# First layer of a four-layer net: half of the shift row and V's shift rows computed by streaming the weights through TensorE, the norm done tile by tile, three weight tiles' products interleaved

## Chip, cores and metric

One core of a Trainium2 chip. The metric is device microseconds (us) of one execution of the whole program, the median of several.

## The reference

A block of two layers (attention with a Hyena mixer, then a pooling layer) is followed by a block of two other layers; all of it is float32, with 512 rows of width 1024 and 256 context rows. The change touches the first layer only, up to the attention scores. Cut to that:

```python
def _modulate(h, shift, scale):
    return h * (1 + scale) + shift
...
    s_lat = jax.nn.silu(c)
    s_ctx = jax.nn.silu(c_ctx)
...
        mod_l = [m[:, None, :] for m in jnp.split(s_lat @ ada_w[i] + ada_b[i], N_MOD, axis=-1)]
        a_lat = _modulate(_rmsnorm(h_lat, norm1_g[i]), mod_l[0], mod_l[1])
...
            mod_c = jnp.split(s_ctx @ ada_w[i] + ada_b[i], N_MOD, axis=-1)
            a_ctx = _modulate(_rmsnorm(h_ctx, norm1_g[i]), mod_c[0], mod_c[1])
...
            p_lat = a_lat @ mix_w_in[e] + mix_b_in[e]
            q_l = _axial_rope(_split_q(p_lat), row, col)
            k_l, v_l = _split_kv(p_lat[..., KV_START:HY_START])
            k_l = _axial_rope(k_l, row, col)
...
            att_l = _diff_post(_diff_attn_blocked(q_l, k_all, v_all, lam), subln_g[e], lam_init)
            hy_l = _hyena(p_lat[..., HY_START:], hy_conv_w[e], hy_conv_b[e], _hyena_filter(seq_len, *filt), hy_bias[e])
```

So a row "shift" of 1024 numbers, once for the 512 rows (c) and once for the context (c_ctx), comes from a vector of 1024 times a 1024 x 1024 matrix. Q, K, V and the Hyena inputs come from the normed rows, the scores from Q and K after the rope.

## The kernel before, in words

The program is one long list of work that the class `Prog` writes out in order for each engine; each engine takes its own instructions in that order, and waits where an operand isn't there. PE multiplies, ACT scales, casts and evacuates PE's banks, VectorE (DVE in the profile, `V` in the code) and GpSimd (POOL, `G`) do the rest, SP issues the transfers. A table `PR` says which of V, G and A (ACT, with POOL adding) does an operation, and how many steps of a side job are put in at each place.

Weights come through six raw tiles of 128x1024. `_dma_to` (line 226, transfers at L233) issues them in a fixed order; `_done_part` asks for the one six places on, once the writing of one tile's last user is behind. A weight tile is cast by ACT to its high part (L255), and the rest is its low part (L273, on V or G by `PR` or `l_eng`). `prefetch` and `consume` put these operations out ahead of the products by `look` parts. A product of float32 accuracy is three matmuls in the fast type, high by high, low by high, high by low (`mm3`, L458 to L460). The modulation rows of later places (`_ada_step`) stand between the weights in the same stream: rows scaled by a column of numbers (`scaled`, L371 on POOL, L373 on ACT) and added (`add_scaled`, L378 on V, L383 on POOL).

The first layer begins with `start`. Its eight column strips of the modulation matrix give the scale `gg` (L1015). `groups` multiplies each of eight tiles of the input, scaled by `gg`, with V's weights (V before its row factors and its shift), 18 matmuls a tile. Side jobs are put between the groups: `hyena_hidden` (two small products with a sine), `first_shift`, and `hyena_filter`. `first_shift` makes the shift: all 16 half rows of eight raw tiles are scaled and added up into four accumulators (two halves, c and c_ctx), the first half on POOL, of the second the c part on V and the c_ctx part by ACT and POOL; then 32 matmuls with a column of ones (L1104) sum over the partitions, and two additions give `sh` (L1107).

The norm comes next. The row factor is broadcast and copied to SBUF; V multiplies eight tiles by it (L1120), ACT applies scale and shift to give the high part (L1129), POOL or V computes the same again (L1130), V takes the difference as low part (L1124). The eight context tiles go the same way at half the width (L1141 to L1144). `v_shift` then makes V's row of shift times weights on V and on ACT and POOL (L378, L383, steps set by `vsj`), broadcasts it with a matmul by ones (L1169), adds the bias (L1170), and adds the row to V's six tiles (L1181).

In `layer0`, Q's first tile is multiplied and roped; then for j = 0 to 3 a K tile is multiplied with the rows and then with the context, and roped. `rope` evacuates the bank on ACT (L1462), shuffles on V (L1463), multiplies by the tables (L1465, L1466) and adds (L1467). The stacking of a K (`stack`, casts and differences L1438 to L1446) is put off by one `defer`. `fj` puts in steps of the Hyena filter (its low parts L527, its products L619), `vsj` steps of `v_shift`. Behind the loop come the scores (L1500, L1505), whose maxima V takes (L1501), for s = 0, 1 and so on, with the other Q and Hyena products between them.

## Time and profile before

| | us |
|---|---|
| median of 3 runs | 2603.05 (2602.36 to 2605.51) |
| the profiled execution | 2603.6 |
| its span in the trace | 2601.4 |
| PE busy | 2455.8 (94%) |
| DVE busy | 1798.1 (69%) |
| POOL busy | 1393.9 (54%) |
| ACT busy | 1178.6 (45%) |
| the stretch up to 437 us: PE / DVE busy | 333.65 / 382.69 |
| behind it (2164.40 us): PE / DVE busy | 2122.11 / 1415.43 |

The span is the time from the first to the last instruction in the trace; the run's time has 2.2 us more around it. A busy time is the sum of an engine's instructions, waits not counted. Matmuls are pipelined, so their starts tell more than their durations. The granted clock is TensorE's, as a share of 2.4 GHz (0.50 is 1.2 GHz).

### The profile page before, as it was taken

Reading aid. Unit: us, or ns where it says so; the run is one execution under the profiler, and the core shown is the slowest. Engines: PE = TensorE matmul, PEld = TensorE weight load, DVE = VectorE, ACT = ScalarE, POOL = GpSimd, SP = SyncE. Lnnn points to the kernel's source line nnn. Section 1 sums busy time; section 2 is a strip of 40 time slices with the busy share of each in tenths; the row PEclk is TensorE's granted clock in tenths of the full one; section 3 lists DMA queues with packets and bytes.
Section 4 is the critical chain, followed back from the end, with each engine's and each line's share of the span. In section 5 each row is a group of like instructions: output and inputs, shape, how many; then the busy total and the mean of one; then the engine's idle time right before and its main releaser. Section 6 shows DMA issues by size and latency. Waiting matters only on the chain.

```text
span 2601.4 us, 31958 instructions
## 1 busy us (share of the span) xinstructions
PE 2455.8 (94%) x11496; PEld 2053.2 (79%) x11496; DVE 1798.1 (69%) x2614; ACT 1178.6 (45%) x2180; POOL 1393.9 (54%) x1104
## 2 busy tenths in 40 slices
PE   7787887999999899999999999999999999999998
PEld 6566666888888788888778888888887788888887
DVE  6899987786656787766678776455477876743334
ACT  3446553554443633333676644222257764523131
POOL 6686747287761389973475437878137544230001
PEclk9888998999999999999999999999999999999999
DMA  7232423276782267663322326667333123343331
GB/s 247 85 122 89 136 69 96 69 208 201 203 235 82 58 171 212 213 197 92 91 67 63 105 86 191 187 173 209 107 91 91 53 82 115 114 139 96 95 89 49
DMA packets 433366, 330.28 MB, mean 127 GB/s; under 512 B 11799, under 2 KB 365207, under 8 KB 433208
## 3 DMA queue, kind: packets, MB, share of 16 engines
q1 hardware_dynamic: 429976, 322.22, 41.6%
q0 software_dynamic: 3232, 6.03, 0.8%
q8 instruction: 90, 1.47, 0.2%
q14 instruction: 68, 0.56, 0.1%
HBM read 319.82 MB, written 8.39 MB: 126 GB/s over the span
## 4 chain that ended last, share of the span: by engine, by line
PE 73%; DVE 16%; ACT 5%; issue 3%; DMA 2%; POOL 2%; SPq 0%; DVEq 0%; ACTq 0%; POOLq 0%
PE ps L458 21%; PE ps L459 20%; PE ps L460 20%; PE ps L619 4%; PE ps L477 3%; DVE slot L273 1%; DVE slot L2049 1%; DVE slot L1553 1%; PE pss L574 1%; PE ps L1385 1%; DVE mx L1501 1%; DVE slot L1527 1%; ACT slot L2046 1%; DMA raw<-in_ada_w_dram 1%; DVE slot L1984 1%
## 5 line engine op out<-in xcount | busy, mean ns | idle before, releaser
L458 PE MATMUL ps<-slot 128*128 128x512 f32 (+1 forms) x3024 | 1164.2, 385 | 37.7 <-DVE slot L2166 14.1
L460 PE MATMUL ps<-slot 128*128 128x512 f32 (+1 forms) x3024 | 1155.1, 382 | 21.5 <-DVE slot L527 9.2
L459 PE MATMUL ps<-slot 128*128 128x512 f32 (+1 forms) x3024 | 1155.6, 382 | 5.9 <-POOL slot L273 3.5
L458 PEld LDWEIGHTS ps<-slot 128*128 128x128 f32 x3024 | 580.5, 192 | 150.8 <-DVE slot L2166 16.3
L460 PEld LDWEIGHTS ps<-slot 128*128 128x128 f32 x3024 | 579.8, 192 | 132.1 <-DVE slot L527 9.5
L459 PEld LDWEIGHTS ps<-slot 128*128 128x128 f32 x3024 | 580.5, 192 | 111.1 <-POOL slot L273 4.6
L383 POOL TENSOR_TENSOR slot<-slot 128x512 f32<-128x512 f32 x336 | 489.5, 1457 | 126.7 <-ACT slot L373 101.0
L255 ACT CAST slot<-raw 128x512 fp32r<-128x512 f32 (+1 forms) x764 | 425.9, 612 | 269.4 <-DMA raw<-in_mlp_w_dram 150.9
L273 DVE TENSOR_TENSOR slot<-raw,slot 128x512 fp32r<-128x512 f32 x588 | 501.6, 897 | 25.9 <-ACT slot L255 24.6
L542 POOL TENSOR_TENSOR slot<-slot 128x512 f32<-128x512 f32 (+1 forms) x64 | 90.8, 1422 | 509.1 <-ACT slot L536 493.7
L273 POOL TENSOR_TENSOR slot<-raw,slot 128x512 fp32r<-128x512 f32 (+1 forms) x176 | 249.2, 1443 | 149.5 <-ACT slot L255 99.9
L371 POOL TENSOR_SCALAR slot<-raw,cols 128x512 f32<-128x512 f32 x192 | 201.2, 1051 | 118.0 <-DMA raw<-in_w_ada_dram 83.7
L536 ACT ACTIVATE slot<-slot 128x512 f32<-128x512 f32 (+1 forms) x98 | 55.3, 576 | 224.6 <-DVE slot L1716 69.8
L619 PE MATMUL ps<-slot 128*128 128x512 f32 x576 | 146.3, 414 | 6.1 <-DVE slot L1821 6.1
L371 POOL TENSOR_SCALAR slot<-raw,s_lat 128x512 f32<-128x512 f32 x96 | 114.0, 1191 | 61.7 <-DMA raw<-in_ada_w_dram 23.3
L2216 DVE TENSOR_TENSOR slot<-slot,ps 128x512 f32<-128x512 f32 x40 | 27.5, 688 | 170.6 <-PE ps L460 170.6
L619 PEld LDWEIGHTS ps<-slot 128*128 128x128 f32 x576 | 114.7, 201 | 31.8 <-DVE slot L1821 7.4
L526 ACT CAST slot<-slot 128x512 fp32r<-128x512 f32 x80 | 47.7, 619 | 182.9 <-DVE slot L2216 154.0
L477 PE MATMUL ps<-slot 128*128 128x512 f32 x480 | 110.2, 389 | 0.0
L477 PEld LDWEIGHTS ps<-slot 128*128 128x128 f32 x480 | 90.0, 188 | 18.6
L1716 DVE SCALAR_TENSOR_TENSOR slot<-ps,mod,slot 128x512 f32<-128x512 f32 x64 | 47.7, 746 | 81.2 <-PE ps L460 81.2
L2241 DVE SCALAR_TENSOR_TENSOR slot<-ps,mod,slot 128x512 f32<-128x512 f32 x40 | 30.0, 749 | 101.7 <-PE ps L460 101.7
(324 smaller groups left out, 2763.6 us busy)
## 6 DMA issues: line engine op xcount, KB each, us to landing
raw<-in_mlp_w_dram SPq DMA_DIRECT2D x128, 512.0 KB, 5.2
raw<-in_w_ada_dram SPq DMA_DIRECT2D x96, 512.0 KB, 4.6
raw<-in_ada_w_dram SPq DMA_DIRECT2D x88, 512.0 KB, 4.7
raw<-in_w_ffn_in_dram SPq DMA_DIRECT2D x88, 512.0 KB, 4.8
raw<-in_w_in_dram SPq DMA_DIRECT2D x56, 512.0 KB, 3.8
raw<-in_w_ffn_out_dram SPq DMA_DIRECT2D x32, 512.0 KB, 4.7
raw<-in_mix_w_dram SPq DMA_DIRECT2D x20, 512.0 KB, 3.9
raw<-in_w_out_dram SPq DMA_DIRECT2D x16, 512.0 KB, 3.9
```

Source lines behind the costliest of these rows:

```text
L255: self.S.copy(r(v), src[:, k:k + kk, :])
L273: eng.tensor_tensor(r(lv), src, v, op=ALU.subtract)
L371: self.G.tensor_scalar(out, x, sc, 0.0, op0=ALU.mult, op1=ALU.add)
L383: self.G.tensor_tensor(out, out, v, op=ALU.add)
L458: self.PE.matmul(out, lhsT=wh, rhs=xh, start=start, stop=False)
L459: self.PE.matmul(out, lhsT=wl, rhs=xh, start=False, stop=False)
L460: self.PE.matmul(out, lhsT=wh, rhs=xl, start=False, stop=stop)
L477: self.PE.matmul(ps[:], lhsT=w[k][i], rhs=xs[k][j], start=(k == 0 and n == 0), stop=(k == kc - 1 and n == 2))
L526: self.S.copy(r(h)[:, 0:n], src)
L536: self.S.activation(sq[:, 0:n], x, AF.Square, scale=scale)
L542: (eng or self.G).tensor_tensor(st["acc"][:, 0:n], st["acc"][:, 0:n], sq[:, 0:n], op=ALU.add)
L619: PE.matmul(ps[:], lhsT=w[i][:, m * 128:(m + 1) * 128], rhs=r(x[j])[:], start=(k == 0 and n == 0), stop=(k == 7 and n == 2))
```

## The change

`first_shift` now works in two ways. For the first half of the shift, `wide` copies the 16 columns of silu(c) and silu(c_ctx), each 32 times, to a 128x512 tile; `two_rows` multiplies the raw tiles' eight rows of tiles by it on PE, as float32, so that the bank holds the sum for c on partitions 0 to 31 and for c_ctx on 32 to 63. ACT copies the bank, four small matmuls with columns of `ident` turn it back into columns, and V adds the bias. The second half is scaled by ACT and added by POOL for both vectors, then summed with ones as before. `start` takes the first step before the strips, and no longer sums anything behind the groups. The norm reads the broadcast row factor from the bank, and goes tile by tile: V multiplies, ACT gives the high part, ACT (even tiles) or V (odd ones) the same again, V the low part. `prefetch` ahead of it goes to three parts, and to four ahead of the context tiles. `v_shift` uses `wide` and `two_rows` on the eight tiles of V's weights, and broadcasts each of the two rows with a matmul. In `layer0` Q's first tile and the first two K tiles are multiplied together, step by step (`keys`), with the first step of `v_shift` behind them; the ropes of Q, K0, K1 and K2 follow, and the K loop does the context products and the stacking. K3 is consumed in the loop at j = 3. `PR` moves the steps of the side jobs, Q's low parts to V, and two additions of `va` to POOL.

```diff
-    l_q='G',
+    l_q='V',
...
-    fs='GGVA',
-    vs='VA',
-    fstep=(1, 2, 1, 0, 0, 1, 0, 3),
-    side=(6, 1, 9, 0),
+    fstep=(0, 0, 1, 3, 1, 1, 0, 1),
+    side=(6, 1, 5, 0),
...
-    va='VGVVVV',
+    va='VGVGVG',
...
-    vsj=(2, 1, 0, 1),
-    fj=(1, 2, 0, 2),
+    vsj=(0, 1, 1, 1),
+    fj=(3, 1, 2, 2),
...
-    def first_shift(self):
...
+    def wide(self, cols):
+        t = self.get()
+        self.V.tensor_copy(t[:].rearrange("p (a b) -> p a b", b=32),
+                           cols[:].rearrange("p k (c o) -> p (k c) o", o=1).to_broadcast([128, 16, 32]))
+        return t
+    def two_rows(self, ps, wide, ws):
+        for k, w in ws:
+            self.PE.matmul(ps[0:64, :], lhsT=wide[:, k * 64:(k + 1) * 64], rhs=w, start=(k == 0), stop=(k == 7))
+    def first_shift(self, sh):
+        V, PE = self.V, self.PE
+        bias = lambda half: self.col("ada_b", 4 * half, 4)
+        def part():
+            p = self.parts[self.cur][0]
+            self.cur_h = self.cur_l = self.cur = self.cur + 1
+            return p
+        s2 = self.wide(self.s2)
+        yield
+        ps, o = self.ps_s.tile([128, 512], F32, tag="pss", name="pss"), self.get()
+        for i in range(4):
+            p = part()
+            self.two_rows(ps, s2, [(2 * i + kk, p["raw"][:, kk, :]) for kk in range(2)])
+            self._done_part(p)
+        self.S.copy(o[0:64, :], ps[0:64, :])
+        self.put(s2)
+        yield
+        ps = self.ps_s.tile([128, 512], F32, tag="pss", name="pss")
+        for k in range(4):
+            PE.matmul(ps[:, 2 * k:2 * k + 2], lhsT=o[0:64, k * 128:(k + 1) * 128], rhs=self.ident[0:64, 0:64:32], start=True, stop=True)
+        self.put(o)
+        for c in range(2):
+            V.tensor_tensor(sh[:, 0:4, c], ps[:, c:8:2], bias(0), op=ALU.add)
+        yield
+        acc = [self.get(), self.get()]
+        for i in range(4):
+            p = part()
+            for kk in range(2):
+                k = 2 * i + kk
+                for c, o in enumerate(acc):
+                    (self.scaled if k == 0 else self.add_scaled)("A", o[:], p["raw"][:, kk, :], self.s2[:, k, c:c + 1])
+            self._done_part(p)
+            yield
+        ps = self.ps_s.tile([128, 512], F32, tag="pss", name="pss")
+        for c, o in enumerate(acc):
+            for k in range(4):
+                PE.matmul(ps[:, 4 * c + k:4 * c + k + 1], lhsT=o[:, k * 128:(k + 1) * 128], rhs=self.ones[:, 0:1], start=True, stop=True)
+        for c in range(2):
+            V.tensor_tensor(sh[:, 4:8, c], ps[:, 4 * c:4 * c + 4], bias(1), op=ALU.add)
+        self.put(acc)
+        yield
...
+        SP.dma_start(out=self.ident[:], in_=a["cst"][:, 0:128])
         self._dma_to(5)
-        SP.dma_start(out=self.ident[:], in_=a["cst"][:, 0:128])
...
+        next(shift)
...
-        bp, rb = self.bcast(y, 4, self.ps_s, "pss"), self.get()
...
+        self.prefetch(3)
         self.vt = []
         def out(i):
             S.activation(t[:], pss[i][:], AF.Copy, scale=y[:, i:i + 1])
             self.vt.append(t)
+        def norm(x, f, n, c_, hi, lo, k):
+            t, z = self.get(), self.get()
+            sc, b = gg[:, k, c_:c_ + 1], sh[:, k, c_:c_ + 1]
+            V.tensor_tensor(t[:, 0:n], x, f, op=ALU.mult)
+            S.activation(r(hi), t[:, 0:n], AF.Identity, scale=sc, bias=b)
+            if k % 2:
+                V.tensor_scalar(z[:, 0:n], t[:, 0:n], sc, b, op0=ALU.mult, op1=ALU.add)
+            else:
+                S.activation(z[:, 0:n], t[:, 0:n], AF.Identity, scale=sc, bias=b)
+            V.tensor_tensor(r(lo), z[:, 0:n], hi, op=ALU.subtract)
+            self.put(t, z)
+        A, AC = [], []
+        bp = self.bcast(y, 4, self.ps_s, "pss")
         for i in range(2):
             out(i)
-        A, AC = [], []
-        self.l_eng = G
         for k in range(8):
-            self.eng("ax").tensor_tensor(xs[k][:], xs[k][:], rb[:], op=ALU.mult)
...
+            hl = self.pair()
+            norm(xs[k][:], bp[:], T, 0, hl[0][:], hl[1][:], k)
             A.append(hl)
             self.put(xs[k])
-            low(t, hl)
-        self.put(rb)
-        for i in range(2, 6):
+            if k in (2, 4):
+                out(1 + k // 2)
+        bp = self.bcast(y[:, 4:6], 2, self.ps_s, "pss")
+        for i in range(4, 6):
             out(i)
-        for _ in range(8 - 2 * len(PR["tapk"])):
-            next(self.filt)
+        self.prefetch(4)
         for k in range(8):
-            t, p = self.get(), self.get()
-            self.eng("cx").tensor_tensor(cx[k], cx[k], rc[:, 0:TC], op=ALU.mult)
-            S.activation(r(p)[:, 0:TC], cx[k], AF.Identity, scale=gg[:, k, 1:2], bias=sh[:, k, 1:2])
-            self.eng("ct").tensor_scalar(t[:, 0:TC], cx[k], gg[:, k, 1:2], sh[:, k, 1:2], op0=ALU.mult, op1=ALU.add)
-            self.eng("cl").tensor_tensor(r(p)[:, TC:2 * TC], t[:, 0:TC], p[:, 0:TC], op=ALU.subtract)
+            p = self.get()
+            norm(cx[k], bp[:, 0:TC], TC, 1, p[:, 0:TC], p[:, TC:2 * TC], k)
             AC.append(p)
-            self.put(t)
-        self.put(rc)
+        self.put(cxt)
         self.sh = sh
-        self.put(cxt)
-        next(self.filt)
         self.vw = vw
...
-        V, G, S = self.V, self.G, self.S
+        V, PE = self.V, self.PE
+        wide, rows = self.wide(self.sh), self.get()
+        ps = self.ps_s.tile([128, 512], F32, tag="pss", name="pss")
+        self.two_rows(ps, wide, [(k, self.vw[k][:]) for k in range(8)])
+        self.S.copy(rows[0:64, :], ps[0:64, :])
+        self.put(self.vw, wide)
+        yield
         acc = [self.get(), self.get()]
-        for k in range(8):
...
         for c, o in enumerate(acc):
             ps = self.ps_s.tile([128, 512], F32, tag="pss", name="pss")
-            self.PE.matmul(ps[:], lhsT=self.ones[:], rhs=o[:], start=True, stop=True)
+            PE.matmul(ps[:], lhsT=self.ident[0:64, 32 * c:32 * c + 1].to_broadcast([64, 128]), rhs=rows[0:64, :], start=True, stop=True)
             V.tensor_tensor(o[:], ps[:], self.bv[:], op=ALU.add)
-        self.put(self.bv)
-        self.VV = [None] * 6
+        self.put(rows, self.bv)
+        self.VV, hs = [None] * 6, []
         yield
-        hs = []
...
-        zq(0, gemm1("q"))
+        look, self.look = self.look, 0
+        ws, ropes = [self.consume(n) for n in ("q", "k", "k", "k")], []
+        def keys(ws):
+            pss = [self.ps() for _ in ws]
+            for k in range(8):
+                for w, ps in zip(ws, pss):
+                    self.mm3(ps[:], w[k], axs[k], k == 0, k == 7)
+            return pss
+        pss = keys(ws[0:3])
+        next(vs)
+        self.put(ws[0].tiles)
+        zq(0, pss[0])
+        for j in range(2):
+            ropes.append(self.rope(pss[1 + j], bin_(4 + j), rope))
+        ropes.append(self.rope(keys(ws[3:4])[0], bin_(6), rope))
         self.l_eng = V
         KL, KC = [], []
         for j in range(4):
-            w = self.consume("k")
-            ps, pc = self.ps(), self.ps()
-            for k in range(8):
-                self.mm3(ps[:], w[k], axs[k], k == 0, k == 7)
+            if j == 3:
+                self.look = look
+                ws.append(self.consume("k"))
+                ropes.append(self.rope(keys(ws[4:5])[0], bin_(7), rope))
+            w, pc = ws[1 + j], self.ps()
             for k in range(8):
                 self.mm3(pc[:, 0:TC], w[k], acs[k], k == 0, k == 7)
             self.put(w.tiles)
-            a = self.rope(ps, bin_(4 + j), rope)
+            a = ropes[j]
```

Three places where the order of the work differs follow; each row is one instruction, or several alike (x).

ACT's queue behind the last context tile, before (L526 are casts of the Hyena filter, L255 of weights, L1462 the ropes' evacuations, L1237 those of the context K):

```order
L1142 ACTIVATE slot<-slot,sh,gg 128x256 x8
L526 CAST slot<-slot 128x512 x6
L255 CAST slot<-raw 128x512 x2
L1462 ACTIVATE slot<-ps,cols 128x512
L255 CAST slot<-raw 128x512 x2
L1462 ACTIVATE slot<-ps,cols 128x512
L1237 ACTIVATE slot<-ps,cols 64x256 x2
```

The same place after (L1182 is the copy of V's two rows, L1497 the ropes' evacuations, L524 the filter's casts, L253 those of weights, L1583 the high parts of V):

```order
L1144 ACTIVATE slot<-slot,sh,gg 128x256
L1182 COPY slot<-pss 64x512
L1497 ACTIVATE slot<-ps,cols 128x512 x4
L1272 ACTIVATE slot<-ps,cols 64x256 x2
L1473 CAST slot<-slot 64x512
...
L524 CAST slot<-slot 128x512 x6
L1583 CAST slot<-slot 128x512 x2
L253 CAST slot<-raw 128x512 x6
L1497 ACTIVATE slot<-ps,cols 128x512
```

The copy of V's rows stands ahead of four rope evacuations in a row, and the casts of the last K tile stand far behind, right ahead of its own rope.

DVE's queue at the end of the context norm, before (L1143 and L1144 are the norm, L527 the filter's low parts, L273 those of a weight, L1463 and L1465 the rope):

```order
L1143 TENSOR_SCALAR slot<-slot,gg,sh 128x256
L1144 TENSOR_TENSOR slot<-slot 128x256
L527 TENSOR_TENSOR slot<-slot 128x512 x4
L273 TENSOR_TENSOR slot<-raw,slot 128x512 x2
L1463 STREAM_SHUFFLE slot<-slot 128x512
L1465 TENSOR_TENSOR slot<-slot 128x512
```

And after (L940 is the widened copy of the shift that V's product reads, L1498 and L1500 the rope):

```order
L1143 TENSOR_TENSOR slot<-slot,pss 128x256
L1146 TENSOR_SCALAR slot<-slot,gg,sh 128x256
L1149 TENSOR_TENSOR slot<-slot 128x256
L940 COPY slot<-sh 128x512
L1498 STREAM_SHUFFLE slot<-slot 128x512
L1500 TENSOR_TENSOR slot<-slot 128x512
```

The first shuffle follows the widened copy at once, where low parts stood between before.

POOL's queue behind the norm, before (L1466 and L1467 are the rope, L383 additions, L371 scaled rows of the next modulation):

```order
L1466 TENSOR_TENSOR slot<-slot 128x512
L1467 TENSOR_TENSOR slot<-slot 128x512
L383 TENSOR_TENSOR slot<-slot 128x512 x3
L371 TENSOR_SCALAR slot<-raw,s_lat 128x512 x2
L383 TENSOR_TENSOR slot<-slot 128x512
L371 TENSOR_SCALAR slot<-raw,s_lat 128x512
```

And after (L1501 and L1502 are the rope, L525 the filter's low parts, L1199 an addition of V's row, L369 and L381 the modulation):

```order
L1501 TENSOR_TENSOR slot<-slot 128x512
L1502 TENSOR_TENSOR slot<-slot 128x512 x2
L525 TENSOR_TENSOR slot<-slot 128x512 x4
L1199 TENSOR_TENSOR slot<-slot 128x512
L369 TENSOR_SCALAR slot<-raw,s_lat 128x512 x2
L381 TENSOR_TENSOR slot<-slot 128x512
...
L381 TENSOR_TENSOR slot<-slot 128x512
L1501 TENSOR_TENSOR slot<-slot 128x512
L1502 TENSOR_TENSOR slot<-slot 128x512
```

The modulation rows start only behind the filter's low parts and an addition of V's row, and all of them (12 scaled rows, 10 additions) stand in one block ahead of the last K's rope.

## Rows read from the trace of the kernel before

**Rows 1.** Stretches: from:to, us long, each engine's busy us (instructions), granted clock, DMA share, GB/s.

```profile
128.00:187.40 59.40, 47.34 (x216) 38.94 (x216) 58.71 (x73) 28.46 (x50) 49.44 (x35) 0.86 0.38 124
175.00:187.40 12.40, 9.10 (x27) 6.95 (x28) 12.20 (x17) 4.82 (x8) 12.07 (x11) 0.69 0.79 252
187.40:230.00 42.60, 31.12 (x127) 24.60 (x125) 37.19 (x56) 24.62 (x59) 28.44 (x23) 0.84 0.23 75
...
270.00:310.00 40.00, 34.87 (x170) 29.21 (x169) 38.90 (x63) 23.84 (x53) 33.50 (x30) 0.90 0.28 92
...
437.00:480.00 43.00, 43.00 (x191) 35.59 (x190) 32.49 (x43) 21.16 (x37) 20.00 (x15) 1.00 0.35 99
480.00:520.00 40.00, 40.00 (x185) 33.41 (x184) 27.20 (x52) 23.75 (x37) 3.97 (x4) 0.96 0.20 56
```

**Rows 2.** Timeline of DVE: start, length, line, operation, count [idle before, releaser].

```profile
88.53 6.49 DVE L378 SCALAR_TENSOR_TENSOR slot<-raw,s,slot 128x512 f32<-128x512 f32 x6
98.68 0.24 DVE L1107 TENSOR_TENSOR sh<-pss,cols 128x8 f32<-128x8 f32 x2 [3.66 <-PE pss L1104]
98.83 4.71 DVE L1120 TENSOR_TENSOR slot<-slot 128x512 f32<-128x512 f32 x7
...
126.82 0.40 DVE L1143 TENSOR_SCALAR slot<-slot,gg,sh 128x256 f32<-128x256 f32 x1
...
127.67 2.49 DVE L527 TENSOR_TENSOR slot<-slot 128x512 fp32r<-128x512 f32 x4
...
131.29 0.01 DVE L1463 LOAD_MASK_SELECT slot<-slot  x1
...
157.83 5.81 DVE L527 TENSOR_TENSOR slot<-slot 128x512 fp32r<-128x512 f32 x4
...
187.49 1.28 DVE L1501 TENSOR_REDUCE mx<-ps 128x1 f32<-128x512 f32 x2
...
195.94 1.28 DVE L1170 TENSOR_TENSOR slot<-pss,slot 128x512 f32<-128x512 f32 x2
197.14 1.28 DVE L1501 TENSOR_REDUCE mx<-ps 128x1 f32<-128x512 f32 x2
```

**Rows 3.** Timeline of ACT, from the scaled rows to the last K.

```profile
73.48 5.00 ACT L373 ACTIVATE slot<-raw,s 128x512 f32<-128x512 f32 x8
...
99.55 5.75 ACT L1129 ACTIVATE slot<-slot,sh,gg 128x512 fp32r<-128x512 f32 x8 [4.35 <-DVE slot L1120]
...
115.65 1.30 ACT L1142 ACTIVATE slot<-slot,sh,gg 128x256 fp32r<-128x256 f32 x2 [0.54 <-POOL slot L1141]
...
172.00 1.14 ACT L255 CAST slot<-raw 128x512 fp32r<-128x512 f32 x2 [12.71 <-DMA raw<-in_mix_w_dram]
173.16 0.69 ACT L1462 ACTIVATE slot<-ps,cols 128x512 f32<-128x512 f32 x1
```

**Rows 4.** Timeline of SP, and the page's DMA issues (KB, us to landing).

```profile
168.12 8.76 SPq L233 DMA_DIRECT2D raw<-in_mix_w_dram  x2
...
raw<-in_mix_w_dram SPq DMA_DIRECT2D x20, 512.0 KB, 3.9
```

**Rows 5.** Timeline of PE: filter, sums of the shift, last K, V's row.

```profile
56.24 0.77 PE L458 MATMUL pss<-slot 128*128 128x512 f32 x1 [10.87 <-DVE gg L1020]
...
95.07 3.57 PE L1104 MATMUL pss<-ones,slot 128*128 128x1 f32 x16 [2.41 <-DVE slot L378]
...
175.26 0.76 PE L458 MATMUL ps<-slot 128*128 128x512 f32 x1 [8.02 <-DVE slot L1240]
175.82 0.63 PE L459 MATMUL ps<-slot 128*128 128x512 f32 x1
176.25 0.63 PE L460 MATMUL ps<-slot 128*128 128x512 f32 x1
...
190.10 1.88 PE L1169 MATMUL pss<-slot,ones 128*128 128x512 f32 x4
```

**Rows 6.** Timeline of POOL, around the ropes and the modulation rows.

```profile
132.09 1.63 POOL L1466 TENSOR_TENSOR slot<-slot 128x512 f32<-128x512 f32 x1 [5.47 <-DVE slot L1463]
...
159.66 3.43 POOL L383 TENSOR_TENSOR slot<-slot 128x512 f32<-128x512 f32 x2
...
182.01 0.70 POOL L371 TENSOR_SCALAR slot<-raw,s_lat 128x512 f32<-128x512 f32 x1
...
185.40 1.62 POOL L1467 TENSOR_TENSOR slot<-slot 128x512 f32<-128x512 f32 x1
```

**Rows 7.** Chain of waits: start, length, what ran.

```profile
36.99 6.83 DMA raw<-in_ada_w_dram
```

**Rows 8.** Groups up to 520 us: line, engine, operation xcount | busy, mean ns | idle before.

```profile
L383 POOL TENSOR_TENSOR slot<-slot 128x512 f32<-128x512 f32 x72 | 104.6, 1453 | 55.4 <-ACT slot L373 50.1
L371 POOL TENSOR_SCALAR slot<-raw,s_lat 128x512 f32<-128x512 f32 x34 | 35.3, 1041 | 19.2 <-PE ps L619 19.2
L1181 DVE TENSOR_TENSOR slot<-slot 128x512 f32<-128x512 f32 x5 | 5.4, 1108 | 0.0
```

More of the change, by code (lines that the diff above doesn't have):

```diff
@@ L937, in hyena_hidden @@
         yield
-    def first_shift(self):
-        for half in range(2):
-            acc = [self.get(), self.get()]
-            for i in range(4):
-                p = self.parts[self.cur][0]
-                self.cur_h = self.cur_l = self.cur = self.cur + 1
-                for kk in range(2):
-                    k = 2 * i + kk
-                    for c, o in enumerate(acc):
-                        sc, w = self.s2[:, k, c:c + 1], p["raw"][:, kk, :]
-                        if k == 0:
-                            self.scaled(PR["fs"][2 * half + c], o[:], w, sc)
-                        else:
-                            self.add_scaled(PR["fs"][2 * half + c], o[:], w, sc)
-                self._done_part(p)
-                if i == 3:
-                    self.first_acc.append(acc)
-                yield
+    def wide(self, cols):
[3 more added lines that the diff above has]
+        return t
@@ L1008, in start @@
         gx, gc, ws = [], [], []
-        hidden, shift, self.first_acc = self.hyena_hidden(z, w1, w2, w3), self.first_shift(), []
+        hidden, shift = self.hyena_hidden(z, w1, w2, w3), self.first_shift(sh)
         def strip(k):
@@ L1094, in start @@
                     next(self.filt)
-        bp, rb = self.bcast(y, 4, self.ps_s, "pss"), self.get()
-        S.copy(rb[:], bp[:])
-        bp, rc = self.bcast(y[:, 4:6], 2, self.ps_s, "pss"), self.get()
-        S.copy(rc[:, 0:TC], bp[:, 0:TC])
-        ps = self.ps_s.tile([128, 512], F32, tag="pss", name="pss")
-        for half, acc in enumerate(self.first_acc):
-            for c_, o in enumerate(acc):
-                for k in range(4):
-                    j = 8 * c_ + 4 * half + k
-                    PE.matmul(ps[:, j:j + 1], lhsT=o[:, k * 128:(k + 1) * 128], rhs=self.ones[:, 0:1], start=True, stop=True)
-            self.put(acc)
-        for c_ in range(2):
-            V.tensor_tensor(sh[:, :, c_], ps[:, 8 * c_:8 * c_ + 8], self.col("ada_b", 0, 8), op=ALU.add)
+        self.prefetch(3)
         self.vt = []
@@ L1115, in start @@
+        A, AC = [], []
+        bp = self.bcast(y, 4, self.ps_s, "pss")
         for i in range(2):
             out(i)
-        A, AC = [], []
-        self.l_eng = G
         for k in range(8):
-            self.eng("ax").tensor_tensor(xs[k][:], xs[k][:], rb[:], op=ALU.mult)
-        self.prefetch(2)
-        def low(t, hl):
-            self.eng("al").tensor_tensor(r(hl[1])[:], t[:], hl[0][:], op=ALU.subtract)
-            self.put(t)
-        for k in range(8):
-            t, hl = self.get(), self.pair()
-            S.activation(r(hl[0])[:], xs[k][:], AF.Identity, scale=gg[:, k, 0:1], bias=sh[:, k, 0:1])
-            self.eng("at").tensor_scalar(t[:], xs[k][:], gg[:, k, 0:1], sh[:, k, 0:1], op0=ALU.mult, op1=ALU.add)
+            hl = self.pair()
+            norm(xs[k][:], bp[:], T, 0, hl[0][:], hl[1][:], k)
@@ L1145, in start @@
             AC.append(p)
-            self.put(t)
-        self.put(rc)
+        self.put(cxt)
         self.sh = sh
-        self.put(cxt)
-        next(self.filt)
         self.vw = vw
@@ L1225, in layer0 @@
         for j in range(4):
-            w = self.consume("k")
-            ps, pc = self.ps(), self.ps()
-            for k in range(8):
-                self.mm3(ps[:], w[k], axs[k], k == 0, k == 7)
+            if j == 3:
[3 more added lines that the diff above has]
+            w, pc = ws[1 + j], self.ps()
             for k in range(8):
```

8 lines of the change are left out of this document (removed).

## The prediction

> **What bounds the kernel now.** I read the busy time by stage first [rows 1]. From 437 us on PE is busy all the time (43.00 of 43.00 us, then 40.00 of 40.00), at a clock of 1.00 and 0.96: what the first layer loses or gains before that reaches the end of the span one for one, since the change does not touch what comes behind. From 128 to 390 us DVE is the busiest engine (58.71 of 59.40 us in the first of these rows, then 87% to 97%), and PE waits within it. So I follow DVE's queue, and ask of each wait what it stands behind.
>
> The timelines of DVE, ACT, PE, POOL and SP give the marks. DVE starts the norm at 98.83, has the last context tile at 127.67, takes the first maximum (s = 0) at 187.49 and the next (s = 1) at 197.14 [rows 2]. ACT waits 12.71 us for a weight tile until 172.00, and only then evacuates the last K product [rows 3]; SP could issue that tile at 168.12 [rows 4]. PE stood idle for 8.02 us because of it [rows 5]. POOL ends its twelfth scaled row of the next modulation at 182.7 and the last K rope at 187 [rows 6].
>
> The profiled execution took 2603.6 us with a span of 2601.4, 0.55 above the median of 2603.05. I add to 2603.6 and take 0.55 off at the end. Less than 0.2% (5.2 us) is no difference that can be measured here.
>
> **1. Up to the norm: -5.2 us.** The first half of the shift leaves POOL, the second leaves DVE. On PE it is eight fp32 products of 512 columns, two instructions each; two such products took four instructions and 1.88 us [rows 5], so 0.94 each at full clock, 7.5 in all, and they wait for raw tiles that land by about 44.5 (chain of waits: the second of them took from 36.99 to 43.83 [rows 7], and a 64 KB load now goes ahead). PE then does the group behind and strip 5 until about 52. ACT's eight scaled rows (5.00 us [rows 3]) now stand ahead of the last sine, so the filter's first product comes at about 63 instead of 56.24 [rows 5], 7 us late. From there less stands in the way: DVE loses six multiply-adds of 6.49 us in 88.53 to 95.0, and the sums that waited for them until 95.07 [rows 2, 5]. POOL has 14 additions at 1.45 [rows 8] plus two stat additions, done by about 85, before the sums. The group products end at about 87.5, and the shift is there at 89.9 instead of 98.9. Six low parts of the weights (0.62 each, the 2.49 us for four of [rows 2]) now stand ahead of the norm: it starts at 93.6 instead of 98.83.
>
> **2. The norm itself: +5.7 us.** Before, DVE, POOL and ACT worked on different tiles. Now each tile goes DVE, ACT, DVE, and the order on DVE lets no tile overlap the next. With 0.62 for a DVE operation and 0.72 for an ACT one (8 in 5.75 us [rows 3]), an even tile (two of ACT) is 2.75 us, an odd one 2.1: 19.4 us for eight, until 113. Two low parts are 1.2. The context tiles (0.40 on DVE [rows 2], 0.5 to 0.6 on ACT [rows 3]) are 1.9 and 1.45: 13.3 us, until 127.5. The widened copy of the shift has no row; a 512-column row operation costs 0.62, and a contended one 1.45 (5.81 for four [rows 2]); I take 0.7, as POOL is idle: 128.2, against 127.67. The three products that go with the tiles keep PE to about 115. This is the part that gains on PE: two K products of some 5.5 us are done early. But PE's next row is the product of V's weights with the copy, so it then idles 13 us.
>
> **3. V's rows: +10.9 us.** Eight fp32 products: 7.5 us at 2.4 GHz and 13.7 at 1.2 (sixteen instructions of twice 0.43). After an idle stretch the rows stand at 1.2 for some 5 us (the products at 175.26 are 0.43 apart [rows 5], and the stage has a granted clock of 0.69 [rows 1]), so I take 9.5, to 137.7. ACT's copy of the result stands ahead of all rope evacuations in its queue, 0.6 and 0.7 us: DVE can shuffle Q at 139.1. Before, DVE went on without a gap at 127.67. So it is 11.4 late, of which 0.5 is from parts 1 and 2.
>
> **4. To the first maximum: -0.2.** Before this took 59.8 us. The order shows 64 DVE operations now, 40 us at 0.62. Two waits come on top. (a) The filter's products need low parts that DVE makes behind the ropes at about 157, and DVE then needs their results behind a V broadcast and a context product: some 8 us. (b) The low part of the last K tile is asked for late, behind these; DVE has it at about 178. On POOL, two low parts and an addition (4.2 us at 1.4) that wait for the filter go before the first modulation rows; six of those (four scaled at 1.04, two additions at 1.45, 7 us [rows 8]) free the two raw tiles that SP must refill before the next weight tile. POOL starts them at 178, SP issues at about 186, landing is 3.9 [rows 4], and ACT's cast of that tile stands ahead of the evacuation of the last K, as at 172.00 [rows 3]. So ACT is at it at 190, DVE passes it at 191, and the seven operations and score products behind it bring the maximum to 198.7: 59.6. Lateness +11.2.
>
> **5. To the second: +4.3.** POOL has 22 rows of modulation ahead of the last K rope: 12 x 1.04 + 10 x 1.45 = 27.0 us [rows 8], from 178 to 205.4, and two for the rope, 208.3. DVE's stacking of that K is ahead of the maximum for s = 1, which comes at 212.7, 14.0 after the first instead of 9.65. Lateness 15.5.
>
> **6. Behind it: -5.7.** Four of five bias additions (1.108 each [rows 8]) and the two V additions (1.28 [rows 2]) are done earlier or on POOL. Lateness 9.8 us; nothing in [rows 1] gives it back before 437, since DVE has only some us of idle per 40. 2603.6 + 9.8 - 0.55 = **2613 us**.
>
> What is free: the changed low parts of Q, two additions moved to POOL (it was idle for a third of the time from 187 to 230 [rows 1]), ident's load a few places earlier.
>
> **A rule against this sum.** Four low parts took 2.49 us while POOL was idle and 5.81 while it worked [rows 2, 6]. From 128 to 187.4 the mean is 0.86 (58.71 us over 73 rows, five of them mask loads of 0.01 [rows 1, 2]). So an emptied POOL is worth 0.24 us on each of 64 operations, 15 us, and I have spent all of it on waits. The Trainium skill (GPSIMD Engine Reference, Key points) says that GpSimd shares its SBUF interfaces with VectorE and contends with instructions that have two SBUF inputs; the trace agrees by these two rows. By that rule alone part 4 is 40 us, not 59.6, and the result is rival A.
>
> **Rivals.** *A, faster.* The waits (a) and (b) are covered, since DVE at 0.62 is early enough with the filter's low parts and POOL's first modulation rows start some 10 us earlier than I think. It decides at the weight tile: if ACT casts it by 177, the maximum comes at about 139.1 + 40 = 179, 8.4 early, and with -5.7 behind it the time is 2589. With 4 us of wait left and 2 of it on POOL it is 2595. For it: POOL is nearly empty from 85 to 165; against: its queue is in order, and the filter's low parts block it. *B, no difference.* Wait (b) is half as long and part 5 is nothing: 2613 - 6 - 4 = 2603. *C, slower still.* V's products run at 1.2 GHz throughout (+4.2), PE falls back to 1.2 in each of its later gaps (12 products at 0.43 instead of 0.23, +2.4 us, twice), and POOL's late rows contend with DVE: 2624.
>
> **How the numbers follow.** Forecast 0.48, C 0.12, B 0.13, A 0.27. The ends of the unknown costs (copy 0.6 to 1.45, V's rows 7.5 to 13.7, wait (a) 4 to 10, wait (b) 4 to 13) put the forecast at 2606 to 2620. The range 2592 to 2624 takes in B, C and A's upper half; outside are A's lower half and a tail above. Faster by over 0.2% is A, 0.27; within 0.2% B, 0.13; slower 0.60.
>
> **What would show it.** Right: PE idle some 13 us ahead of the V product with an end near 137; ACT's copy of V's rows ahead of the first rope; DVE idle about 10 us there and again ahead of the last K's rope, with ACT waiting for the weight tile; first maximum near 199, second near 213; from 437 on the same as before. Wrong: the V product before 120, a first maximum ahead of 187, or a shift that reaches the norm after 99.

## The result, and the profile after

The change makes the kernel slower: 2626.33 us (2624.42 to 2628.85, 4 runs) against 2602.70 in the runs of the kernel before beside them; the ratio is 1.0086, with a 95% interval of 1.0074 to 1.0098, so 19 to 26 us. The forecast was 2613 in a range of 2592 to 2624: the sign is right, the size is not, and the time lies outside the range. The span of the profiled execution is 2623.4 us, 22.0 above that of before.

The stretches of the changed kernel, from the first multiplication of the norm (from:to, us long, busy us of each engine and its instructions, granted clock, DMA share, GB/s):

```profile
99.70:135.10 35.40, 20.76 (x72) 15.63 (x72) 21.55 (x44) 19.43 (x30) 0.00 (x0) 0.74 0.17 53
135.10:146.00 10.90, 10.38 (x22) 3.69 (x23) 0.41 (x4) 1.23 (x3) 0.00 (x0) 0.79 0.00 0
146.00:212.00 66.00, 45.38 (x218) 36.81 (x217) 51.25 (x69) 26.70 (x48) 37.41 (x30) 0.84 0.26 80
212.00:226.90 14.90, 10.35 (x39) 8.12 (x38) 6.44 (x13) 5.75 (x14) 9.91 (x8) 0.77 0.32 107
437.00:480.00 43.00, 36.70 (x201) 32.53 (x202) 29.66 (x54) 14.43 (x25) 35.34 (x27) 0.92 0.32 98
```

The same work in the kernel before (the norm; from the first rope to the first maximum; up to the second maximum):

```profile
98.80:127.70 28.90, 20.50 (x77) 15.06 (x76) 26.23 (x37) 17.33 (x29) 25.32 (x21) 0.79 0.10 30
131.30:187.50 56.20, 45.14 (x211) 37.54 (x211) 55.51 (x69) 26.05 (x45) 49.54 (x35) 0.88 0.40 132
187.50:197.20 9.70, 9.70 (x43) 7.41 (x42) 6.58 (x13) 6.63 (x15) 3.22 (x3) 1.00 0.15 53
```

DVE was busy 91% and 99% of the first two of these; in the changed kernel it is busy 61% of the norm, 0.41 of the next 10.90 us, and 78% of the 66.00 behind. The kernel got slower because DVE, which set the pace, now waits: it has no more work than before in any of these stretches, but takes longer over each. Its timeline shows for whom it waits; these rows answer to [rows 2]:

```profile
96.03 0.23 DVE L990 TENSOR_TENSOR sh<-pss,cols 128x4 f32<-128x4 f32 x2 [2.98 <-PE pss L988]
...
99.79 0.68 DVE L1143 TENSOR_TENSOR slot<-slot,pss 128x512 f32<-128x512 f32 x1
102.06 0.69 DVE L1149 TENSOR_TENSOR slot<-slot 128x512 fp32r<-128x512 f32 x1 [1.59 <-ACT slot L1148]
...
135.06 0.42 DVE L940 COPY slot<-sh 128x512 f32<-128x512 f32 x1
145.97 0.01 DVE L1498 LOAD_MASK_SELECT slot<-slot  x1 [10.49 <-ACT slot L1497]
...
164.88 2.49 DVE L525 TENSOR_TENSOR slot<-slot 128x512 fp32r<-128x512 f32 x4
...
178.00 1.39 DVE L1481 TENSOR_TENSOR slot<-slot 64x512 fp32r<-64x512 f32 x2 [3.55 <-ACT slot L1473]
...
181.62 5.54 DVE L525 TENSOR_TENSOR slot<-slot 128x512 fp32r<-128x512 f32 x4
...
188.09 6.69 DVE L271 TENSOR_TENSOR slot<-raw,slot 128x512 fp32r<-128x512 f32 x6
203.16 0.01 DVE L1498 LOAD_MASK_SELECT slot<-slot  x1 [8.38 <-ACT slot L1497]
...
211.97 1.28 DVE L1536 TENSOR_REDUCE mx<-ps 128x1 f32<-128x512 f32 x2
...
226.85 1.28 DVE L1536 TENSOR_REDUCE mx<-ps 128x1 f32<-128x512 f32 x2
```

The norm begins at 99.79, the first rope at 145.97, the maxima come at 211.97 and 226.85 (before: 98.83, 131.29, 187.49, 197.14 [rows 2]). Behind the 10.49 us stands V's product on PE, and behind the 8.38 us ACT, which waits for the last weight tile as in [rows 3]; POOL has its one block of modulation rows by then (timelines of PE, ACT and POOL of the changed kernel):

```profile
135.62 9.10 PE L947 MATMUL pss<-slot 128*64 128x512 f32 x16 [10.39 <-DVE slot L940]
...
144.77 0.58 ACT L1182 COPY slot<-pss 64x512 f32<-64x512 f32 x1 [10.08 <-PE pss L947]
145.25 1.83 ACT L1497 ACTIVATE slot<-ps,cols 128x512 f32<-128x512 f32 x3
...
201.33 1.14 ACT L253 CAST slot<-raw 128x512 fp32r<-128x512 f32 x2 [9.91 <-DMA raw<-in_mix_w_dram]
...
181.41 2.94 POOL L525 TENSOR_TENSOR slot<-slot 128x512 fp32r<-128x512 f32 x2 [20.76 <-ACT slot L524]
...
211.59 1.61 POOL L381 TENSOR_TENSOR slot<-slot 128x512 f32<-128x512 f32 x1
```

### The profile page after: what moved, and what is told of

It is laid out like the page before. It is cut to its first block, busy times and chain, and to the rows that moved or that the text cites. A ratio compares the mean times of both kernels' runs of the same rounds, so it can differ in the third digit from the quotient of the medians.

```text
span 2623.4 us, 31940 instructions
## 1 busy us (share of the span) xinstructions
PE 2470.0 (94%) x11520; PEld 2053.4 (78%) x11520; DVE 1767.6 (67%) x2614; ACT 1183.7 (45%) x2188; POOL 1319.8 (50%) x1054
## 4 chain that ended last, share of the span: by engine, by line
PE 74%; DVE 13%; ACT 5%; issue 4%; POOL 2%; DMA 2%; SPq 0%; DVEq 0%; ACTq 0%; POOLq 0%
PE ps L456 21%; PE ps L457 20%; PE ps L458 20%; PE ps L617 5%; PE ps L475 4%; DVE slot L271 1%; DVE slot L2084 1%; PE pss L572 1%; PE ps L1420 1%; DVE slot L1588 1%; PE pss L947 1%; DVE mx L1536 1%; DMA slot<-in_ada_w_dram 1%; ACT slot L2081 1%; POOL slot L381 1%
## 5 line engine op out<-in xcount | busy, mean ns | idle before, releaser
L456 PE MATMUL ps<-slot 128*128 128x512 f32 (+1 forms) x3024 | 1163.8, 385 | 44.3 <-DVE slot L2201 14.1
L458 PE MATMUL ps<-slot 128*128 128x512 f32 (+1 forms) x3024 | 1153.1, 381 | 14.1 <-DVE slot L525 9.2
L253 ACT CAST slot<-raw 128x512 fp32r<-128x512 f32 (+1 forms) x764 | 425.5, 612 | 265.0 <-DMA raw<-in_mlp_w_dram 149.8
L381 POOL TENSOR_TENSOR slot<-slot 128x512 f32<-128x512 f32 x322 | 470.0, 1461 | 144.1 <-ACT slot L371 120.4
L271 DVE TENSOR_TENSOR slot<-raw,slot 128x512 fp32r<-128x512 f32 x590 | 510.4, 910 | 24.4 <-ACT slot L253 23.0
L369 POOL TENSOR_SCALAR slot<-raw,cols 128x512 f32<-128x512 f32 x192 | 199.1, 1040 | 120.0 <-DMA raw<-in_w_ada_dram 85.7
L369 POOL TENSOR_SCALAR slot<-raw,s_lat 128x512 f32<-128x512 f32 x96 | 109.8, 1148 | 63.0 <-DMA raw<-in_ada_w_dram 24.6
L524 ACT CAST slot<-slot 128x512 fp32r<-128x512 f32 x80 | 47.8, 619 | 189.1 <-DVE slot L2251 154.1
```

The source lines that it names most:

```text
L253: self.S.copy(r(v), src[:, k:k + kk, :])
L271: eng.tensor_tensor(r(lv), src, v, op=ALU.subtract)
L369: self.G.tensor_scalar(out, x, sc, 0.0, op0=ALU.mult, op1=ALU.add)
L381: self.G.tensor_tensor(out, out, v, op=ALU.add)
L456: self.PE.matmul(out, lhsT=wh, rhs=xh, start=start, stop=False)
L458: self.PE.matmul(out, lhsT=wh, rhs=xl, start=False, stop=stop)
```

## The experiments

All times in one table; the ratio is to the kernel before on the same chip. The last three columns are DVE's start of the first rope and of the first two maxima in the profile.

| run | us | ratio [95%] | rope | max 1 | max 2 |
|---|---|---|---|---|---|
| before (medians of the chips) | 2602.70 to 2604.93 | 1 | 131.3 | 187.5 | 197.1 |
| the change | 2626.33 | 1.0086 [1.0074, 1.0098] | 146.0 | 212.0 | 226.9 |
| e1_v_late | 2628.92 | 1.0088 [1.0073, 1.0103] | 134.8 | 213.9 | 228.8 |
| e2_norm_ahead | 2616.45 | 1.0043 [1.0028, 1.0057] | 132.5 | 198.7 | 213.5 |
| e3_k3_early | 2624.58 | 1.0069 [1.0054, 1.0084] | 146.4 | 207.2 | 224.8 |
| e4_first_before | 2625.73 | 1.0078 [1.0063, 1.0093] | 147.3 | 213.6 | 228.5 |
| e6_v_early | 2618.78 | 1.0053 [1.0038, 1.0068] | 137.3 | 201.7 | 216.5 |
| e7_k3_off_pool | 2625.53 | 1.0077 [1.0060, 1.0093] | 147.2 | 217.5 | 227.4 |
| e8_early_ahead | 2606.07 | 1.0007 [0.9998, 1.0017] | 127.2 | 191.8 | 206.7 |
| e9_four | 2606.28 | 1.0008 [0.9998, 1.0017] | 129.5 | 194.5 | 205.7 |
| e13_early_ahead_k3 | 2610.88 | 1.0029 [1.0018, 1.0041] | 128.1 | 188.5 | 206.1 |
| e10_old_v_early | 2592.08 | 0.9962 [0.9949, 0.9974] | 132.2 | 177.5 | 186.7 |
| e11_old_first_new | 2603.21 | 0.9998 [0.9989, 1.0006] | 128.4 | 184.6 | 194.2 |
| e12_old_both | 2592.68 | 0.9962 [0.9949, 0.9975] | 130.6 | 175.9 | 185.4 |
| e14_products_changed | 2604.09 | 0.9999 [0.9990, 1.0007] | 124.8 | 190.1 | 205.0 |
| e15_norm_ahead_old | 2593.73 | 0.9957 [0.9944, 0.9971] | 132.7 | 178.4 | 187.5 |
| e16_norm_changed_old | 2603.31 | 0.9999 [0.9990, 1.0007] | 145.0 | 190.6 | 199.7 |

### Where V's product stands

e1_v_late takes it behind the ropes:

```diff
         pss = keys(ws[0:3])
-        next(vs)
...
         ropes.append(self.rope(keys(ws[3:4])[0], bin_(6), rope))
+        next(vs)
```

> The widened copy, V's product and its copy on ACT go behind the four ropes. Theory (V's product stands between the norm and the ropes, and DVE's 10.49 us of idle time at 145.97 are pure loss): the first shuffle comes at about 136.5, the first maximum some 9 us earlier (203), time 2617. Rival (the end of this stage is set by POOL's block of modulation rows and the last weight tile, which wait for the filter, not for the ropes): the first maximum stays at 210 to 212, time 2624 to 2627.

The ropes came 11 us earlier, and nothing was won: the first maximum and the time are even a little above the rival's ranges. DVE stood idle a little later for longer, since PE took V's product ahead of the context products (timelines of DVE and PE of e1_v_late):

```profile
159.43 0.69 DVE L1476 TENSOR_TENSOR slot<-slot 64x512 fp32r<-64x512 f32 x1 [13.80 <-ACT slot L1473]
...
145.78 8.87 PE L947 MATMUL pss<-slot 128*64 128x512 f32 x16 [15.67 <-DVE slot L940]
```

So freeing ACT's queue only moved the wait. V's product needs the widened copy, which DVE now made behind the ropes: PE stood idle for 15.67 us until then, and held up the context products for 8.87 us more. This run doesn't separate the two. The shift is there before the norm, and PE idles within the norm, so e6_v_early starts the product there and delays only the copy of its result:

```diff
         bp = self.bcast(y, 4, self.ps_s, "pss")
+        self.sh, self.vw = sh, vw
+        self.vs = self.v_shift()
+        next(self.vs)
...
+        next(self.vs)
         bp = self.bcast(y[:, 4:6], 2, self.ps_s, "pss")
...
         self.two_rows(ps, wide, [(k, self.vw[k][:]) for k in range(8)])
+        yield
         self.S.copy(rows[0:64, :], ps[0:64, :])
```

> V's product goes ahead of the norm's products on PE, right behind the broadcast of the row factors (its widened copy as soon as the shift is there, its copy on ACT behind the eight norm tiles). In e1_v_late the ropes came 11 us earlier, but PE then did V's product (8.9 us) ahead of the context products, and nothing was won. Theory (its 9 us of PE are on the path wherever PE is what is waited for; while the norm runs, PE idles and they are free): first shuffle at 135 to 137, first maximum 201 to 204, time 2615 to 2619. Rival (the path through this stage is not PE's but the filter's and the last weight tile's, which e1_v_late left where they were): first maximum 209 to 212, time 2623 to 2627.

First maximum 201.7, ratio 1.0053 against 1.0086: the place between norm and ropes cost 0.33%, some 9 us. The theory holds. e6_v_early takes away both, PE's 9 us and PE's wait for the copy, so how the 9 us split between them stays open.

### The norm

```diff
             else:
                 S.activation(z[:, 0:n], t[:, 0:n], AF.Identity, scale=sc, bias=b)
+            u = more() if more else None
             V.tensor_tensor(r(lo), z[:, 0:n], hi, op=ALU.subtract)
```

where `more` is the multiplication of the next tile, taken out of the head of `norm`.

> In the norm, the multiplication of the next tile goes ahead of a tile's low part on DVE, so that ACT has work while DVE waits. Theory (the chain DVE, ACT, DVE without overlap costs the 13.4 us that DVE idles between 99.8 and 135.1): the widened copy comes 8 to 13 us earlier, at 122 to 127, and the time falls by about as much, to 2614 to 2618. Rival (the raw tile that casts in the norm wait for, or ACT itself, sets the pace): the copy comes less than 4 us earlier, time 2622 to 2626.

The widened copy comes at 121.91 instead of 135.06, and the time falls by 0.43%, as the theory had it. In the profile 3.4 us of the 13.2 are an earlier shift (92.64 against 96.03, of the same instructions); the norm alone is 25.5 us instead of 35.4 (its first to its last tile in e2_norm_ahead), with nearly the same DVE work, 20.14 against 21.55:

```profile
96.40:121.90 25.50, 20.14 (x72) 15.17 (x72) 20.14 (x43) 18.57 (x30) 0.00 (x0) 0.81 0.23 72
```

### The last weight tile, POOL's block, the new shift

e3_k3_early asks for the last K tile behind the first ropes, e7_k3_off_pool takes two steps of its rope and three additions of V's row from POOL to DVE, e4_first_before has the old `first_shift` with its steps:

```diff
         for j in range(4):
+            if j == 0:
+                self.prefetch(2)
...
-    rope_b='GVVVGGVV',
-    rope_c='GVGVGGGG',
+    rope_b='GVVVVGVV',
+    rope_c='GVGVVGGG',
...
-    va='VGVGVG',
+    va='VVVVVV',
...
-    fstep=(0, 0, 1, 3, 1, 1, 0, 1),
-    side=(6, 1, 5, 0),
+    fstep=(1, 2, 1, 0, 0, 1, 0, 3),
+    side=(6, 1, 9, 0),
```

> A prefetch of two parts stands right behind the first four ropes: the casts and low part of the last K tile and the first half of the modulation rows come ahead of the filter's low parts on ACT, DVE and POOL. Theory (asking late for that tile, and POOL's block behind the filter, cost the 8.38 us of DVE's idle time at 203.16 and the gap of 14.9 us between the first two maxima): the first maximum 8 to 10 us earlier, the second 10 to 15, time 2612 to 2616. Rival (the casts wait for the tile at the head of ACT's queue and hold up what is behind, or POOL's rows delay the filter): time 2626 or more.

> The last K's rope and the additions of V's row go to DVE; POOL's block of 22 modulation rows stays, but nothing of the scores waits for what stands behind it. Theory (the block costs the gap between the first two maxima, 14.9 us against 9.65 before, and ACT's 6.82 us of waiting for POOL's addition at 219.52): gap of 9 to 11 us, time 2619 to 2622. Rival (the longer queue of DVE, or the modulation itself, takes the place): time 2624 to 2628.

> Only first_shift is as it was (accumulators on POOL, V and ACT, sums behind the groups), with the old steps of the side jobs; norm, V's rows and the interleaved products stay changed. Theory (the new shift gains 2.7 us at most, 96.03 against 98.68, and the norm's start lost it to six low parts): 2626 to 2630. Rival (the new shift costs time, because PE takes 6.4 us for its second half and POOL's additions come in late): 2618 to 2623.

e3: the first maximum comes 4.8 us earlier, the second 2.1; the intervals of the ratio overlap with the change's. DVE's wait ahead of the first maximum is gone, and the one ahead of the second is longer than the change's 8.32 us (DVE of e3_k3_early):

```profile
197.41 0.01 DVE L1500 LOAD_MASK_SELECT slot<-slot  x1 [0.53 <-ACT slot L1499]
...
220.93 1.40 DVE L1483 TENSOR_TENSOR slot<-slot 64x512 fp32r<-64x512 f32 x2 [11.06 <-ACT slot L1475]
```

e7: the gap between the maxima falls from 14.9 to 9.9 as expected, but the first comes 5.5 later, and the second stays: what POOL no longer delays, DVE now does itself (from the last K's rope to the first maximum it takes 12.8 us instead of 8.8). Its time is the rival's. Neither theory holds at the end of the span. e4: no difference that the runs can tell, so the new shift is worth about nothing here.

### Together

> e6_v_early and e2_norm_ahead together. Theory (both delays are on one path, one behind the other, so they add): 2605 to 2609. Rival (V's product needs the idle time of PE that the quicker norm takes away): 2611 to 2616.

> e2, e3, e6 and e7 together: multiplication one tile ahead, V's product early, last K tile and half of the modulation rows asked for behind the first ropes, last K's rope and V's additions on DVE. Theory (every named delay is on the path): 2595 to 2603, at or below the kernel before. Rival (with the delays gone, DVE is the bound again as in the kernel before, and it has more work here): 2604 to 2611.

> e8_early_ahead with e3_k3_early's prefetch (the last K's rope and V's additions stay as in the change). Theory (with the two main delays gone, the wait for the last weight tile is still 8 us of DVE's time, as in e8_early_ahead, and e9_four lost it again by putting five additions and two rope steps on DVE): 2601 to 2604. Rival (the wait is covered by what follows, as in e3_k3_early where 4.8 us at the first maximum were 2 us at the end): 2604 to 2607.

e8 has what the theory gave: 0.33% and 0.43% add, and the change is back at the time of the kernel before. e9 gains nothing more, its rival's time. In e13 the first maximum is 3.3 us earlier than in e8 and the second where it was, since the wait moved as in e3: ahead of the first maximum DVE waits 0.53 us instead of 8.30, ahead of the second 11.10 instead of 8.36. Its time is longer than either theory had it, and why is not settled (its profiled span, 2604.2 us, is within 1 us of e8's 2603.3).

### Parts of the change alone, on the kernel before

e10_old_v_early puts the new `v_shift` into the kernel before as in e6_v_early, e11_old_first_new the new `first_shift`, e12_old_both both:

```diff
-    vsj=(2, 1, 0, 1),
+    vsj=(0, 0, 0, 0),
...
+        self.sh, self.vw = sh, vw
+        self.vs = self.v_shift()
+        next(self.vs)
         for i in range(2):
             out(i)
```

> The kernel before, with one part of the change alone, and at another place: V's row by PE (v_shift as in e6_v_early, its product started ahead of the norm's products, its copy on ACT behind the norm's eight tiles). DVE loses eight scaled additions of 0.6 to 1.2 us between 128 and 160, POOL eight additions of 1.5 and ACT eight scalings. Theory (V's row by PE is a gain where PE idles anyway): first maximum 4 to 8 us earlier than in the kernel before, time 2597 to 2601. Rival (9 us of PE ahead of the norm's products make the first Q and K products and so the ropes late by as much): time 2604 to 2612.

> The kernel before with the new first_shift alone (first half by PE, second by ACT and POOL, its steps and the earlier load of ident as in the change). Theory (the new shift brings the norm's start forward by no more than the 2.7 us seen in the change, as the sums wait for the groups on PE): norm's start at 95.5 to 98.5, time 2600 to 2604. Rival (without the six low parts ahead of the norm it is worth the 5.2 us of my sum): 2597 to 2599.

> e10_old_v_early and e11_old_first_new together: both uses of PE for a row, with norm and products as before. Theory (the two add): 2594 to 2600. Rival (PE ahead of the norm is then what is waited for): 2602 or more.

e10 is faster than both kernels, 0.9962 [0.9949, 0.9974], and by more than its theory had: V's row by PE is worth 10 us, if PE has the time for it. DVE, still busy 94% of the stretch of [rows 1], gets through 80 rows in it instead of 73:

```profile
128.00:187.40 59.40, 53.32 (x242) 43.02 (x243) 55.63 (x80) 31.03 (x59) 42.64 (x31) 0.89 0.42 135
```

e11: the shift came at 91.36 and the norm 6.4 us earlier than before (earlier than its theory had it), but the first maximum only 2.9, and the time is the same. e12 adds nothing to e10: it is below both ranges, but the theory that the two add does not hold.

Then what of the change remains, beside V's place and the norm? e12 with either the change's order of products or its norm. The order comes with all that the change ties to it: larger prefetches, other places for the filter's steps, Q's low parts on DVE, two additions of V's row on POOL:

```diff
-        zq(0, gemm1("q"))
+        pss = keys(ws[0:3])
+        self.put(ws[0].tiles)
+        zq(0, pss[0])
...
+            hl = self.pair()
+            norm(xs[k][:], bp[:], T, 0, hl[0][:], hl[1][:], k)
```

> e12_old_both with the change's order of products (Q, K0, K1 together, ropes in a row, the late last K tile, steps of the filter and of V's row as in the change); the norm is as in the kernel before. Theory (the order of the products costs what e8_early_ahead lacks against e12_old_both, through the waits for the filter and the last weight tile): 2603 to 2608, first maximum at 188 to 192 with ropes at 130. Rival (it is the norm): 2591 to 2596.

> e12_old_both with the norm of e2_norm_ahead (tile by tile on DVE and ACT, multiplication one tile ahead); the order of products as in the kernel before. Theory (order of products is the cause; this norm takes DVE no longer than the old one): 2590 to 2595. Rival (the norm costs the rest): 2602 to 2608.

> e12_old_both with the norm as in the change (no multiplication ahead). Theory (the chain without overlap costs what e2_norm_ahead gave back, 10 us): 2600 to 2605. Rival (in the old order the K products are ready later anyway and cover it): 2592 to 2597.

All three have the theory's time. The new order alone takes e12's gain away, and the new norm alone does too, unless it multiplies one tile ahead. In e14 the ropes begin 5.8 us earlier than in e12 and the first maximum comes 14.2 later. ACT waits for the last weight tile in both; in e12 DVE does not stand behind that, in e14 it does, for 8.23 us. Ahead of the second maximum DVE waits in both, but 8.32 us instead of 2.93, behind a cast of ACT's that waits for an addition of POOL's (timelines of ACT and DVE of e12_old_both):

```profile
163.19 1.14 ACT L254 CAST slot<-raw 128x512 fp32r<-128x512 f32 x2 [6.95 <-DMA raw<-in_mix_w_dram]
...
181.16 1.41 DVE L1473 TENSOR_TENSOR slot<-slot 64x512 fp32r<-64x512 f32 x2 [2.93 <-ACT slot L1465]
```

and of e14_products_changed:

```profile
179.31 1.14 ACT L253 CAST slot<-raw 128x512 fp32r<-128x512 f32 x2 [9.76 <-DMA raw<-in_mix_w_dram]
...
181.15 0.01 DVE L1502 LOAD_MASK_SELECT slot<-slot  x1 [8.23 <-ACT slot L1501]
...
197.63 0.62 ACT L1587 CAST slot<-slot 128x512 fp32r<-128x512 f32 x1 [6.82 <-POOL slot L1204]
...
201.10 1.40 DVE L1485 TENSOR_TENSOR slot<-slot 64x512 fp32r<-64x512 f32 x2 [8.32 <-ACT slot L1477]
```

So the 22.4 us (0.86%) come in four steps, by the ratios times 2604: from the kernel before to e12 (both rows by PE, early) -9.9; to e16 (the norm without overlap) +9.6; to e6_v_early (the order of products on top) +14.1; to the change (V's product between norm and ropes) +8.6. Each is uncertain by 3 to 5 us, and the split depends on the order of the steps: the order of products first is +9.6 (e14), the norm on top of it +14.1. How the order's share splits into the weight tile, the filter's low parts and POOL's block is open: the weight tile and POOL's block taken alone moved a wait to another place (e3, e7), and the filter's low parts were not tried alone.

## Why the prediction was wrong

The forecast failed in two steps: PE's time from the filter's first product to the sums of the shift (part 1), and the way from POOL's modulation rows over the weight tile to the last K's rope (part 4).

- **Part 1 (-5.2 forecast).** Failed: the norm began at 99.79, +1.0. The filter's first product came when forecast (62.64, forecast 63), but the group products ended at 94.2 instead of 87.5: 31.5 us, where the forecast had 24.5 and gave no working for it. Of these PE waited 2.1 us, and in two stretches the products stood at half clock, 0.43 apart instead of 0.23, which I estimate at 2.5 and 1.4 us from the distances of the rows. The first lies behind 4.66 us of idle time, the second, up to 91.7, behind a wait for the filter. In the rows of PE, and the two stretches:

```profile
62.64 0.77 PE L456 MATMUL pss<-slot 128*128 128x512 f32 x1 [4.66 <-POOL slot L381]
...
66.20 0.63 PE L457 MATMUL ps<-slot 128*128 128x512 f32 x1
66.63 0.63 PE L458 MATMUL ps<-slot 128*128 128x512 f32 x1
...
87.65 0.50 PE L456 MATMUL pss<-slot 128*128 128x512 f32 x1 [1.14 <-DVE slot L873]
...
89.63 0.63 PE L456 MATMUL ps<-slot 128*128 128x512 f32 x1
90.05 0.63 PE L457 MATMUL ps<-slot 128*128 128x512 f32 x1
...
94.16 1.84 PE L988 MATMUL pss<-ones,slot 128*128 128x1 f32 x16
```

```profile
62.60:70.90 8.30, 7.25 (x20) 5.42 (x21) 5.03 (x5) 1.04 (x2) 3.66 (x3) 0.50 0.54 182
87.60:91.80 4.20, 4.15 (x12) 3.23 (x13) 3.83 (x13) 1.85 (x5) 1.77 (x2) 0.61 0.02 7
```

In e2_norm_ahead, with the same instructions up to there, the second wait was 0.30 us and the granted clock behind it 1.00, and the way still took 29.9 us (60.82 to 90.77). So the second stretch varies with the execution, and most of the miss does not. The other profiles of the same front part have the shift at 92.6 to 97.3; and where the 5 us were really won (e11), the end of the span got nothing of them.
- **Part 2 (norm 34.6 until the copy).** Right: 35.3, though PE's three products ended at 125.2 and not at 115, so PE idled 10.4 us instead of 13. e16 and e15 show that this term, which I had booked as +5.7, costs 10 at the end.
- **Part 3 (from the copy to the first rope, 10.9).** Right: 10.9, with V's product at 9.1 instead of 9.5. But the queue of ACT, in which I saw the cost, was not all of it: e1_v_late freed it, the ropes came 11 us earlier, and nothing was won while V's product and its copy stood ahead of the context products.
- **Part 4 (59.6 from rope to maximum).** Mis-sized, 66.0. The waits of DVE were 14.8 us instead of 19.6, but its own operations took 0.80 us, 51.2 in all, where I had 0.62 and 40 (the count of 64 is right: 69 rows with five mask loads). My price is that of an idle POOL, and by part 5 of the forecast itself POOL works from 178 on: the low parts of the filter took 2.49 us at 164.88 and 5.54 at 181.62, beside POOL's own at 181.41. The Trainium skill (GPSIMD Engine Reference, Key points) states this contention; the trace agrees by these two rows. I weighed the rule for the stage as a whole, and did not ask which part of it POOL would fill.

Yet that price made the stage longer only in small part. DVE is through with its low parts at 194.8 and then waits 8.38 us for ACT, which waits for the weight tile; with cheaper operations it would have waited longer. The way that set the end is the one that I had as wait (b), and its terms were too small. POOL began its modulation rows 40.0 us after the first rope (forecast 38.9). Four scaled rows and two additions took 9.4 us instead of 7, since scaled rows took 1.6 us beside DVE's low parts and 0.69 once DVE was idle. SP issued the tile at 195.84, and ACT cast it 5.5 us later instead of 4; DVE's rope came 1.8 us behind that instead of 1, the maximum 8.8 behind the rope instead of 7.7. That is +1.1, +1.9, +1.5, +0.8 and +1.1, the 6.4 us (timelines of POOL and SP):

```profile
185.99 3.26 POOL L369 TENSOR_SCALAR slot<-raw,s_lat 128x512 f32<-128x512 f32 x2
...
196.70 0.69 POOL L369 TENSOR_SCALAR slot<-raw,s_lat 128x512 f32<-128x512 f32 x1
...
195.84 1.05 SPq L231 DMA_DIRECT2D raw<-in_mix_w_dram  x2
```

- **Part 5 (14.0 between the maxima).** Right: 14.9.
- **Part 6 (-5.7 behind).** Nearly: 29.7 us late at the second maximum, 22.0 at the end of the span. PE is busy without a gap somewhat later than 437 us, 36.70 of 43.00 up to 480.
- **The rivals.** A's mechanism, the waits covered, did not happen, nor did B's: part 5 was 14.9 us and not nothing. C came nearest, with 2624. Its clock in V's product was not the miss (9.1 us, not 13.7); its other two conditions are in the trace, PE at half clock behind a later gap (products 0.43 apart from 189.4 to 194.1, behind 9.59 us of idle time) and POOL's rows beside DVE's. The misses of parts 1 and 4 (6.2 and 6.4 us) make 12.6 of the 13.3 us by which the time exceeds the forecast. The other parts nearly cancel. The range failed because its bounds were those of DVE's waits and of V's product; neither PE's time in the groups nor POOL's rows and the tile behind them had any.

## What to carry to other kernels

Work given to an idle engine is free only at the time at which that engine idles: V's row by TensorE is a gain of 10 us ahead of the norm and was lost between the norm and the products that DVE waits for. Moving work behind a wait doesn't take it off the path if another engine waits for the same one next; look who is waited for, not only whose queue it stands in. And an operation that gets dearer costs nothing while its engine waits for something else right behind it: follow the way that ends last. An element-wise chain over two engines wants the next tile's first step ahead of this tile's last, or each engine pays for the other.
